# The odd layer's output projection: eight block products of its last 1024 columns against seven on sums of blocks

## The chip, the cores and the metric

The kernel runs on one core of a Trainium2 chip. The metric is device time in microseconds of one launch. Engine names are those of the profile: PE multiplies matrices (PEld loads its stationary operand), DVE, ACT and POOL work element by element (VectorE, ScalarE, GpSimd), and SP only issues transfers.

## The reference, cut to what matters

The reference is a two-layer encoder on 256 tokens of width 2048: an even layer with two attention branches, an odd layer with windowed attention, and a final norm. The change touches the last lines of the odd layer and the norm behind it:

```python
y = yc.reshape(b, s, C_WIDTH) * jax.nn.silu(gate)
h = h + jnp.einsum('bse,ed->bsd', y, w_out_odd[i])
...
return rms_norm(h, final_norm_g)
```

Here `y` is 256 x 2048 (tokens by features), `w_out_odd` is 2048 x 2048, and the norm divides each token's 2048 values by their root mean square and multiplies by a gain vector.

## The kernel before

Every projection is a *job*: 512 output columns for both halves of the tokens (`t` = 0, 1; 128 tokens each), accumulated over 16 feature tiles of 128 in two PSUM banks. A product in float32 accuracy is three matmuls (`mm3`, lines 186 to 188): each operand is held as a rounded high part and a low rest, and high*high, high*low and low*high are summed. So a job of 512 columns is 2 x 16 x 3 = 96 matmuls of 512 columns.

The weights come from memory as float32. `wgroup` (lines 131 to 150) loads one group, 128 x 1024 values (two feature tiles of 512 columns), into one of three `raw` buffers, ACT rounds it to `hi` (line 147) and DVE subtracts, `lo = raw - hi` (line 148). I call that pair a *split*. `hi` and `lo` have three buffers each, so ACT can begin the split of a group when PE has finished the group three places earlier. Each group feeds 12 matmuls.

The attention of the odd layer runs as small tasks between the groups. At the end of a head pair, `finish` multiplies the pair's outputs `o` by the gate (line 405), and splits them into the stationary operands `y[k]`, one for each of the 16 feature tiles. The output projection needs all of them, and the last four come late, so `two_jobs` (lines 211 to 217) runs columns 0 to 511 and 512 to 1023 side by side: the first six groups of both, then the last two of both. Sixteen groups in all; I number them w1 to w16 in the order in which PE takes them.

Behind them follow the columns 1024 to 1535 as a job of eight groups, the columns 1536 to 1791 as a job with 256 columns a matmul, and the columns 1792 to 2047 from weights split into tiles of the free activation pool `u`, once for each half of the tokens. After each job `final_add` (lines 744 to 749) adds the two PSUM banks to the residual stream `tok` on DVE, squares and sums it on ACT (line 244), and multiplies by the gain on DVE. When a token half has all its columns, lines 767 to 780 form the reciprocal root (one `pow` on POOL), scale the row on DVE and ACT, and write it out.

POOL issues the small transfers that turn activations by 128 (`turned`, line 287), and adds the attention bias tables (lines 425 and 427). Its last real work before the output projection is the `turned` transfers of the last two head pairs; in the output projection it has only the two `pow`.

The order on each engine is chosen at build time by the framework's scheduler from the program order; `tc.high_priority()` moves an instruction ahead of others, and `behind()` keeps an instruction behind the newest split.

## Time and profile before

| quantity | value |
|---|---|
| device time, median of 3 runs | 876.97 us (876.04 to 877.44) |
| device time of the profiled execution | 876.38 us |
| its span in the trace | 874.5 us |
| PE busy | 862.5 us, 99% |
| DVE busy | 650.9 us, 74% |
| ACT busy | 531.5 us, 61% |
| POOL busy | 283.4 us, 32% |
| granted PE clock, mean | 0.998 |

The span runs from the first to the last instruction of the trace; the launch around it is 1.9 us in the profiled execution, and the median of the runs is 0.6 us above that execution. Busy shares count an instruction from its start to its end, also while it waits for a port, and matmuls overlap each other, so a PE at 99% is one that is never without work, not one that has no faster way through it.

### The profile page before, as it was taken

The page shows a single profiled execution, that of the slowest core. Times are in us where ns is not written, and L with a number is a line of the kernel's source. Part 1 is how long each engine was busy: PE and PEld are TensorE (multiplying, and loading weights), DVE is VectorE, ACT ScalarE, POOL GpSimd, SP SyncE. Part 2 cuts the span into 40 slices and gives each one's busy share as a digit, 9 for nine tenths or more (in the row PEclk, how much of TensorE's full clock was granted, in tenths as well). Part 3 has the DMA queues.
Part 4 walks back from the last instruction along what each step waited for, and adds up shares of the span by engine and source line. Part 5 has one row for each costly group of instructions (what it writes and reads, how often), then busy time and mean ns, then how long its engine had stood idle before and what let it go on. Part 6 is the DMA issues. An engine that isn't in the chain of part 4 may idle for free. (4 is left out here: it accounts for less than half of the span.)

```text
span 874.5 us, 12145 instructions
## 1 busy us (share of the span) xinstructions
PE 862.5 (99%) x4068; PEld 722.8 (83%) x4068; DVE 650.9 (74%) x925; ACT 531.5 (61%) x882; POOL 283.4 (32%) x417
## 2 busy tenths in 40 slices
PE   8999999999999999999999999999999999999996
PEld 7788888888888888888888888888888888878896
DVE  6598879977997996786567875587658767785664
ACT  7755878769756964465455754475546655664542
POOL 0033323451555650322031732164115622450000
PEclk9999999999999999999999999999999999999999
DMA  8877564684667676667575666666665575576562
GB/s 299 296 260 241 184 228 160 205 263 165 193 195 250 218 247 213 197 223 255 197 229 183 219 214 217 212 196 217 214 219 193 183 245 175 186 259 233 192 203 108
DMA packets 58431, 187.75 MB, mean 215 GB/s; under 512 B 11072, under 2 KB 11840, under 8 KB 58368
## 3 DMA queue, kind: packets, MB, share of 16 engines
q1 hardware_dynamic: 46656, 162.57, 55.4%
q0 software_dynamic: 11712, 24.40, 9.3%
q8 instruction: 32, 0.52, 0.3%
q14 instruction: 31, 0.25, 0.1%
HBM read 161.50 MB, written 2.10 MB: 187 GB/s over the span
## 5 line engine op out<-in xcount | busy, mean ns | idle before, releaser
L148 DVE TENSOR_TENSOR lo<-raw,hi 128x1024 fp32r<-128x1024 f32 (+1 forms) x294 | 363.0, 1239 | 181.3 <-ACT hi L147 180.9
L147 ACT ACTIVATE hi<-raw 128x1024 fp32r<-128x1024 f32 (+1 forms) x294 | 309.4, 1053 | 266.1 <-PE acc_t L188 194.5
L187 PE MATMUL acc_t<-lo,u 128*128 128x512 f32 x928 | 361.3, 391 | 1.8 <-DVE lo L148 1.7
L188 PE MATMUL acc_t<-hi,u 128*128 128x512 f32 x928 | 360.5, 390 | 0.0
L186 PE MATMUL acc_t<-hi,u 128*128 128x512 f32 x928 | 332.7, 391 | 1.2 <-ACT u L232 1.2
L287 POOL DMA_DIRECT2D pt<-x x356 | 194.0, 596 | 329.4 <-DVE x L283 97.4
L187 PEld LDWEIGHTS acc_t<-lo,u 128*128 128x128 f32 x928 | 174.4, 188 | 38.2 <-DVE lo L148 3.9
L186 PEld LDWEIGHTS acc_t<-hi,u 128*128 128x128 f32 x928 | 173.3, 188 | 36.4 <-ACT u L232 2.3
L188 PEld LDWEIGHTS acc_t<-hi,u 128*128 128x128 f32 x928 | 174.4, 188 | 34.6
L187 PE MATMUL acc_t<-lo,y 128*128 128x512 f32 (+1 forms) x256 | 95.9, 376 | 0.0
L188 PE MATMUL acc_t<-hi,y 128*128 128x512 f32 (+1 forms) x256 | 95.8, 376 | 0.0
L425 POOL TENSOR_SCALAR bias<-geo 128x512 f32<-128x512 f32 x24 | 49.4, 2058 | 122.0 <-DVE s L420 115.4
L186 PE MATMUL acc_t<-hi,y 128*128 128x512 f32 (+1 forms) x256 | 87.0, 376 | 0.0
L188 PEld LDWEIGHTS acc_t<-hi,y 128*128 128x128 f32 x256 | 48.2, 188 | 8.7
L187 PEld LDWEIGHTS acc_t<-lo,y 128*128 128x128 f32 x256 | 48.1, 188 | 8.6
L186 PEld LDWEIGHTS acc_t<-hi,y 128*128 128x128 f32 x256 | 48.1, 188 | 8.6
L283 DVE STREAM_TRANSPOSE x<-z 128x256 f32<-128x256 f32 x82 | 45.0, 602 | 0.1
L283 DVE STREAM_TRANSPOSE x<-s 128x256 f32<-128x256 f32 x64 | 37.2, 620 | 7.4 <-ACT s L498 5.9
L368 ACT ACTIVATE s<-s,nm 128x256 f32<-128x256 f32 x64 | 31.7, 496 | 5.0 <-DVE nm L365 4.8
L265 ACT ACTIVATE z<-acc_t,rstd 128x512 f32<-128x512 f32 x40 | 27.0, 676 | 5.4 <-PE acc_t L188 5.3
L258 ACT ACTIVATE ph<-pt 128x512 fp32r<-128x512 f32 x32 | 19.9, 623 | 14.7 <-DMA pt<-x 14.6
L772 POOL TENSOR_TENSOR r<-r,nhalf 128x1 f32<-128x1 f32 x2 | 1.4, 679 | 78.8 <-DVE r L771 78.8
(138 smaller groups left out, 704.4 us busy)
## 6 DMA issues: line engine op xcount, KB each, us to landing
raw<-in_w_in_odd SPq DMA_DIRECT2D x128, 512.0 KB, 3.9
raw<-in_w_in_even SPq DMA_DIRECT2D x102, 512.0 KB, 3.8
pt<-x POOLq DMA_DIRECT2D x356, 64.0 KB, 3.5
raw<-in_w_out_even SPq DMA_DIRECT2D x32, 512.0 KB, 4.3
raw<-in_w_out_odd SPq DMA_DIRECT2D x32, 512.0 KB, 3.2
tok<-in_x SPq DMA_DIRECT2D x4, 512.0 KB, 8.3
xk<-in_xt SPq DMA_DIRECT2D x6, 256.0 KB, 5.2
raw<-in_w_in_even SPq DMA_DIRECT2D x4, 256.0 KB, 4.0
```

Source lines behind the costliest of these rows:

```text
L147: firsts.append(A.activation(hi[:, ks], rv[:, ks], AF.Copy))
L148: splits.append(V.tensor_sub(lo[:, ks], rv[:, ks], f(hi[:, ks])))
L186: T.matmul(ps, ah, bh, start=start, stop=False)
L187: T.matmul(ps, ah, bl, start=False, stop=False)
L188: T.matmul(ps, al, bh, start=False, stop=stop)
L258: A.activation(hi, src, AF.Copy)
L265: A.activation(z[:, t], ps[t], AF.Copy, scale=r[:, t:t + 1])
L283: V.transpose(x[:, :, 2 * m:2 * m + 2].rearrange("p b t c -> p t b c"), src[:, :, m * P:(m + 1) * P].rearrange("p t (r b) -> p t b r", b=4))
L287: G.dma_start(dst[:, a].rearrange("p n c -> p (n c)"), x[32 * a:32 * a + 32].rearrange("r b n c -> r (b n c)"))
L368: A.activation(e[:, t], s[:, t], AF.Exp, bias=nm[:, t:t + 1], accum_out=den[:, t:t + 1])
L425: G.tensor_scalar_mul(b, geo[:, 0], -slope)
L772: G.tensor_tensor(r, r, nhalf[:, :1], op=ALU.pow)
```

## The change

The columns 1024 to 2047 no longer run as three jobs. They are one product of 256 tokens x 2048 features with 2048 features x 1024 columns, cut into 2 x 2 blocks: tokens in two halves of 128, features in two halves of 1024, columns in two halves of 512. Three of the four pairs of feature tiles in each half (index `j` = 0, 1, 2) go through the seven-product scheme of Strassen and Winograd; the fourth pair of each half (feature tiles 6, 7, 14 and 15) is multiplied as before and closes the sums.

For each `j`, `strassen` loads four weight blocks of 128 x 1024 values (`b11`, `b12`, `b21`, `b22`) and makes seven right-hand sides: `b11`, `b21`, `b22` as they are, and four sums: `t1 = b12 - b11` (POOL), `t3 = b22 - b12` (POOL), `t3 + b11`, written over `b22` (DVE), and `b21` less that sum, written over `b21` (POOL). Each of the seven is split like a group before (ACT rounds, DVE subtracts) and feeds 6 matmuls of 512 columns. The left-hand sides are blocks of `y` or four sums of them (`left_forms`), made from the gated outputs `o` by four DVE instructions of 128 x 256 and one split of 128 x 1024 for each `j`; they are made while the first two jobs run, in the pool `u`.

The products' banks are added to `tok` when the last `j` is done: product 1 to both column halves of token half 0 by one DVE instruction; product 6 to one block by DVE; the other contributions by eight POOL additions of 128 x 512 from copies that ACT takes out of PSUM (`add_behind`). Products 2, 3 and 4 stay open and take the fourth pairs. The gain multiplication of columns 0 to 1535 moves from DVE to POOL (six instructions of 128 x 512), and that of columns 1536 to 2047 is merged into the last scaling on DVE. The weights of the first two `j` are loaded into attention tiles that are free by then. The gain vector's four transfers are issued after the twelfth group instead of before the first.

```diff
-CHUNKS_E = ((0, 512), (512, 512), (1024, 512), (1536, 512))
-CHUNKS = ((0, 512), (512, 512), (1024, 512), (1536, 256), (1792, 256))
+CHUNKS = ((0, 512), (512, 512), (1024, 512), (1536, 512))
...
-    def two_jobs(w, c0, c1, a, late=(6, 7)):
+    def two_jobs(w, c0, c1, a, late=(6, 7), between=None):
 
         ps = [job_banks(512) for _ in range(2)]
         for kgs in ([kg for kg in range(8) if kg not in late], late):
             for p, c in zip(ps, (c0, c1)):
                 job_steps(p, w, c, 512, a, kgs, last=2 * late[-1] + 1)
+            if kgs is not late and between:
+                between()
...
+    def left_forms(dst, a1, a2):
+        s = work.tile([P, 4, 2, P], F32, tag="z", name="s4", bufs=3)
+        a11, a21, a12, a22 = a1[:, :, :P], a1[:, :, P:], a2[:, :, :P], a2[:, :, P:]
+        V.tensor_add(s[:, 0], a21, a22)
+        V.tensor_sub(s[:, 1], s[:, 0], a11)
+        V.tensor_sub(s[:, 2], a11, a21)
+        V.tensor_sub(s[:, 3], a12, s[:, 1])
+        sv = s.rearrange("p f k c -> p f (k c)")
+        split(dst[:, :, 0], dst[:, :, 1], sv)
+    def strassen(wb, c0, c1, a, left, done):
+        w, where = wb
+        def load(c, kg, pool, tag, bufs):
+            dst = pool.tile([P, 1024], F32, tag=tag, name=f"w_{tag}", bufs=bufs)
+            loads.append(nc.sync.dma_start(dst, w[where[c] + kg]))
+            return dst
+        def load_three(j):
+            b11 = load(c0, j, heads, ("va", "ka")[j % 2], 1)
+            b12 = load(c1, j, heads, "k", 2)
+            b21 = load(c0, 4 + j, heads, "q", 2)
+            return b11, b12, b21
+        def first_form(b11, b12):
+            t1 = work.tile([P, 1024], F32, tag="z", name="t1", bufs=3)
+            with tc.high_priority():
+                G.tensor_sub(t1, b12, b11)
+            return t1
+        def parts_of(src):
+            count[0] += 1
+            if count[0] % 4:
+                hi = wpool.tile([P, 2, 512], F32R, tag="hi", name="hi")
+                lo = wpool.tile([P, 2, 512], F32R, tag="lo", name="lo")
+            else:
+                both = heads.tile([P, 2, 2, 512], F32R, tag="v", name="both", bufs=1)
+                hi, lo = both[:, 0], both[:, 1]
+            sv = src.rearrange("p (k c) -> p k c", k=2)
+            with tc.high_priority():
+                firsts.append(A.activation(hi, sv, AF.Copy))
+                splits.append(V.tensor_sub(lo, sv, f(hi)))
+            return hi, lo
+        count = [0]
+        three = load_three(0)
+        t1_next = first_form(*three[:2])
+        yield
+        b22_next = load(c1, 4, wpool, "raw", 3)
+        with tc.high_priority():
+            G.tensor_sub(three[1], b22_next, three[1])
+        ps = {i: bank() for i in (1, 2, 3, 5)}
+        ps.update({i: acc.tile([P, 512], F32, tag="acc", name=f"acc_s{i}") for i in (6, 7, 4)})
+        for j in range(3):
+            (b11, t3, b21), t1, b22 = three, t1_next, b22_next
+            def block(k0, t):
+                return lambda kk, i: a[k0 + 2 * j + kk][:, i, t * P:(t + 1) * P]
+            def form(n):
+                return lambda kk, i: left[j][:, n - 1, i, kk * P:(kk + 1) * P]
+            def product(i, lhs, rhs):
+                hi, lo = parts_of(rhs)
+                for kk in range(2):
+                    mm3(ps[i], lhs(kk, 0), lhs(kk, 1), hi[:, kk], lo[:, kk], j == kk == 0, i not in (2, 3, 4) and j == 2 and kk == 1)
+                if j == 2 and i not in (2, 3, 4):
+                    done(i, ps[i])
+            three = load_three(j + 1)
+            product(1, block(0, 0), b11)
+            product(2, block(8, 0), b21)
+            product(3, form(4), b22)
+            with tc.high_priority():
+                V.tensor_add(b22, t3, b11)
+                G.tensor_sub(b21, b21, b22)
+            b22_next = load(c1, 5 + j, wpool, "raw", 3)
+            if j < 2:
+                t1_next = first_form(*three[:2])
+            product(5, form(1), t1)
+            if j < 2:
+                with tc.high_priority():
+                    G.tensor_sub(three[1], b22_next, three[1])
+            product(7, form(3), t3)
+            product(6, form(2), b22)
+            product(4, block(8, 1), b21)
+        b11, b12, b21 = three
+        blocks = {b: parts_of(src) for b, src in (((0, 0), b11), ((1, 0), b21), ((0, 1), b12), ((1, 1), b22_next))}
+        end = {(0, 0): ps[2], (0, 1): ps[3], (1, 0): ps[4],
+               (1, 1): acc.tile([P, 512], F32, tag="acc", name="acc_s8")}
+        newest = None
+        for t, n in ((0, 0), (0, 1), (1, 0), (1, 1)):
+            for half in range(2):
+                hi, lo = blocks[half, n]
+                for kk in range(2):
+                    ak = a[8 * half + 6 + kk][:, :, t * P:(t + 1) * P]
+                    with tc.issue_after(newest.ins) if newest else nullcontext():
+                        newest = mm3(end[t, n], ak[:, 0], ak[:, 1], hi[:, kk], lo[:, kk],
+                                     t == n == 1 and half == kk == 0, half == kk == 1)
+            done((t, n), end[t, n])
...
+        gated[h // 2] = o
...
-    parts = small.tile([P, NT, 5], F32, tag="parts5", name="parts5", bufs=1)
-    gf = [acts.tile([P, 512], F32, tag="y", name="gf") for _ in range(4)]
-    for c in range(4):
-        G.dma_start(gf[c], final_g[c * 512:(c + 1) * 512].unsqueeze(0).to_broadcast([P, 512]))
-    def gfs(cs):
-        return gf[cs.start // 512][:, cs.start % 512:cs.start % 512 + cs.stop - cs.start]
-    def final_add(i, t, cs, ps, scaled=True):
+    parts = small.tile([P, NT, 4], F32, tag="parts4", name="parts4", bufs=1)
+    gf = []
+    def load_gf():
+        for c in range(4):
+            gf.append(acts.tile([P, 512], F32, tag="y", name="gf"))
+            G.dma_start(gf[c], final_g[c * 512:(c + 1) * 512].unsqueeze(0).to_broadcast([P, 512]))
+    forms = [None] * 3
+    def task_forms(j):
+        yield from until(lambda: gated[j] is not None and gated[j + 4] is not None)
+        yield 1
+        forms[j] = acts.tile([P, 4, 2, S], F32R, tag="u", name="forms", bufs=NK // UG)
+        with behind():
+            left_forms(forms[j], gated[j], gated[j + 4])
+    for j in range(3):
+        spawn(task_forms(j))
+    def columns_done(i, t, cs):
         z = tok[:, t, cs]
+        square_sum(parts[:, t, i:i + 1], z)
+        if i < 3:
+            G.tensor_mul(z, z, gf[cs.start // 512])
+    CS = slice(1024, 1536), slice(1536, 2048)
+    def rows_done(t):
+        ms = small.tile([P, NT], F32, tag="ss", name="ms")[:, :1]
+        V.reduce_sum(ms, parts[:, t, 0:3], axis=AX.X)
+        V.tensor_scalar(ms, ms, 1.0 / D, NORM_EPS, op0=ALU.mult, op1=ALU.add)
+        columns_done(3, t, CS[1])
+        r = small.tile([P, 8], F32, tag="r", name="r", bufs=2)[:, :1]
+        V.tensor_scalar(r, parts[:, t, 3:4], 1.0 / D, ms[:, 0:1], op0=ALU.mult, op1=ALU.add)
+        G.tensor_tensor(r, r, nhalf[:, :1], op=ALU.pow)
+        for c in (3, 0, 2, 1):
+            cs = slice(512 * c, 512 * c + 512)
+            z = tok[:, t, cs]
+            if c == 3:
+                V.scalar_tensor_tensor(z, z, r[:, 0:1], gf[c], op0=ALU.mult, op1=ALU.mult)
+            elif c == 2:
+                V.tensor_scalar_mul(z, z, r[:, 0:1])
+            else:
+                A.activation(z, z, AF.Copy, scale=r[:, 0:1])
+            nc.sync.dma_start(out2[t * P:(t + 1) * P, cs], z)
+    def add(t, n, ps):
+        z = tok[:, t, CS[n]]
         V.tensor_add(z, z, ps)
-        square_sum(parts[:, t, i:i + 1], z)
-        if scaled:
-            V.tensor_mul(z, z, gfs(cs))
-    for i, cs, ps in jobs_out(w_oo, CHUNKS[:4], y):
-        for t in range(NT):
-            final_add(i, t, cs, ps[t])
...
+    def add_both(t, ps):
+        z = tok[:, t, 1024:].rearrange("p (n c) -> p n c", n=2)
+        V.tensor_add(z, z, ps.unsqueeze(1).to_broadcast([P, 2, 512]))
+    def add_behind(ps, blocks):
+        m = work.tile([P, 512], F32, tag="s", name="m", bufs=3)
+        A.copy(m, ps)
+        for t, n in blocks:
+            z = tok[:, t, CS[n]]
+            G.tensor_add(z, z, m)
+    def product_done(i, ps):
+        if i == 1:
+            add_both(0, ps)
+            add_behind(ps, ((1, 0), (1, 1)))
+        elif i == 5:
+            add_behind(ps, ((0, 1), (1, 1)))
+        elif i == 7:
+            add_behind(ps, ((1, 0), (1, 1)))
+        elif i == 6:
+            add(0, 1, ps)
+            add_behind(ps, ((1, 0), (1, 1)))
+        else:
+            t, n = i
+            add(t, n, ps)
+            if n:
+                rows_done(t)
             else:
+                columns_done(2, t, CS[0])
+    steps = strassen(w_oo, 1024, 1536, y, forms, product_done)
+    for i, (cs, ps) in enumerate(zip((slice(0, 512), slice(512, 1024)), two_jobs(w_oo, 0, 512, y, between=lambda: (load_gf(), next(steps))))):
+        for t in range(NT):
+            V.tensor_add(tok[:, t, cs], tok[:, t, cs], ps[t])
+            columns_done(i, t, cs)
+    advance(lambda: all(x is not None for x in forms))
+    for _ in steps:
+        pass
```

Three places show what moved. In the rows that follow, `raw`, `w_raw`, `w_va`, `w_ka`, `w_k` and `w_q` are weight blocks as they were loaded, `t_7761` and its like are `t1`, `m` is a copy of a product's bank, and line numbers are those of the kernel they come from (the split of `wgroup` is L148 before and L147 after; that of `strassen` is L272).

POOL, from the last bias table of the attention to the end of the program, before:

```order
L427 TENSOR_TENSOR bias<-bias,geo 128x512
L287 DMA pt<-x 128x1x128 x12
L739 DMA gf<-in_final_norm_g 128x512 x4
L287 DMA pt<-x 128x1x128 x8
L772 TENSOR_TENSOR r<-r,nhalf 128x1 x2
```

POOL, from the same transfers to the eight additions, after:

```order
L395 DMA pt<-x 128x1x128 x20
L258 TENSOR_TENSOR t_7761<-w_k,w_va 128x1024
L258 TENSOR_TENSOR t_7901<-w_k,w_ka 128x1024
L853 DMA gf<-in_final_norm_g 128x512 x4
L281 TENSOR_TENSOR w_k<-w_raw,w_k 128x1024
L313 TENSOR_TENSOR w_k<-w_raw,w_k 128x1024
L871 TENSOR_TENSOR tok<-tok,gf 128x512 x4
L306 TENSOR_TENSOR w_q<-w_q,w_raw 128x1024
L258 TENSOR_TENSOR t_7982<-w_k,w_va 128x1024
L313 TENSOR_TENSOR w_k<-w_raw,w_k 128x1024
L306 TENSOR_TENSOR w_q<-w_q,w_raw 128x1024 x2
L909 TENSOR_TENSOR tok<-tok,m 128x512 x8
```

An engine that had two one-column instructions left now has nine of 128 x 1024 and twelve of 128 x 512 in these rows, and two more multiplications by the gain behind them, all with two inputs in SBUF.

DVE in the first two jobs, from the split of w3 to those of w5 to w7, before:

```order
L148 TENSOR_TENSOR lo<-raw,hi 128x1024
L405 TENSOR_TENSOR o<-o,pt 128x512
L274 SCALAR_TENSOR_TENSOR z<-th,z 128x512
L283 STREAM_TRANSPOSE x<-z 128x2x4x32 x4
L148 TENSOR_TENSOR lo<-raw,hi 128x1024
L259 TENSOR_TENSOR y<-o,y 128x256 x2
L148 TENSOR_TENSOR lo<-raw,hi 128x1024 x3
```

DVE in the same stretch, from the split of w3 to those of w5 and w6 (`s_7530` and `s_7538` are the sums for `j` = 0 and 1), after:

```order
L147 TENSOR_TENSOR lo<-raw,hi 128x1024
L234 TENSOR_TENSOR s_7530<-o,s_7530 128x256
L514 TENSOR_TENSOR o<-o,pt 128x512
L382 SCALAR_TENSOR_TENSOR z<-th,z 128x512
L147 TENSOR_TENSOR lo<-raw,hi 128x1024
L231 TENSOR_TENSOR s_7538<-o 128x256
L391 STREAM_TRANSPOSE x<-z 128x2x4x32 x4
L367 TENSOR_TENSOR forms<-s_7530,forms 128x4x256
L367 TENSOR_TENSOR y<-o,y 128x256 x2
L232 TENSOR_TENSOR s_7538<-s_7538,o 128x256
L147 TENSOR_TENSOR lo<-raw,hi 128x1024 x2
```

Three small instructions of the left-hand sums and the split of those for `j` = 0 (into `forms`) stand between the splits of w3 and w5; four more small ones stand ahead of w3, in rows not shown.

DVE from the last split of the first two jobs on, before:

```order
L746 TENSOR_TENSOR tok<-tok,acc_t_7481 128x512
L746 TENSOR_TENSOR tok<-tok,acc_t_7482 128x512
L148 TENSOR_TENSOR lo<-raw,hi 128x1024
L749 TENSOR_TENSOR tok<-tok,gf 128x512 x2
L148 TENSOR_TENSOR lo<-raw,hi 128x1024
```

DVE from the same additions on, after:

```order
L933 TENSOR_TENSOR tok<-tok,acc_t_7473 128x512
L933 TENSOR_TENSOR tok<-tok,acc_t_7474 128x512
L272 TENSOR_TENSOR lo<-w_va,hi 128x1024
L272 TENSOR_TENSOR lo<-w_q,hi 128x1024
L933 TENSOR_TENSOR tok<-tok,acc_t_7475 128x512
L933 TENSOR_TENSOR tok<-tok,acc_t_7476 128x512
L272 TENSOR_TENSOR lo<-w_raw,hi 128x1024
L305 TENSOR_TENSOR w_raw<-w_k,w_va 128x1024
L272 TENSOR_TENSOR lo<-w_k,hi 128x1024
L272 TENSOR_TENSOR lo<-w_raw,hi 128x1024
L272 TENSOR_TENSOR both<-w_ka,both 128x1024
L272 TENSOR_TENSOR lo<-w_q,hi 128x1024 x2
```

Where a split stood for 12 matmuls there is now one for six, and one sum of weight blocks for each `j` between them.

## Rows read from the trace of the kernel before

**Rows 1.** The page, part 1: busy time, share of span, instructions.
```profile
PE 862.5 (99%) x4068; PEld 722.8 (83%) x4068; DVE 650.9 (74%) x925; ACT 531.5 (61%) x882; POOL 283.4 (32%) x417
```

**Rows 2.** Windows (stretch, length, busy by engine, PEclk, DMA share, GB/s).
```profile
777.20:821.50 44.30, 44.30 (x199) 36.77 (x198) 31.00 (x39) 23.51 (x34) 4.40 (x9) 1.00 0.67 233
821.50:843.30 21.80, 21.80 (x98) 18.06 (x97) 12.25 (x13) 9.83 (x12) 0.00 (x0) 1.00 0.57 194
866.50:874.50 8.00, 0.00 (x0) 0.00 (x0) 2.24 (x6) 1.23 (x3) 0.67 (x1) 0.77 0.42 153
```

**Rows 3.** Chain that ended last (start us, us, what): group beginnings, fifteen groups apart.
```profile
799.91 0.45 PE acc_t L186 x2
...
840.71 0.45 PE acc_t L186 x2
```

**Rows 4.** Timeline of PE (start, us, instruction): 256-column pace, last matmul.
```profile
850.10 0.28 PE L186 MATMUL acc_t<-hi,y 128*128 128x256 f32 x1
...
850.46 0.28 PE L186 MATMUL acc_t<-hi,y 128*128 128x256 f32 x1
...
866.18 0.28 PE L188 MATMUL acc_l<-u,y 128*128 128x256 f32 x1
```

**Rows 5.** Timeline of PE: the first matmuls of w5.
```profile
788.87 0.62 PE L186 MATMUL acc_t<-hi,y 128*128 128x512 f32 x2
789.32 0.39 PE L187 MATMUL acc_t<-lo,y 128*128 128x512 f32 x1
```

**Rows 6.** Timeline of DVE in the first two jobs: splits of w2, w3, w5/w6, w16.
```profile
777.30 1.23 DVE L148 TENSOR_TENSOR lo<-raw,hi 128x1024 fp32r<-128x1024 f32 x1 [0.24 <-ACT hi L147]
778.44 0.76 DVE L259 TENSOR_TENSOR y<-o,y 128x256 fp32r<-128x256 f32 x2
...
780.10 1.23 DVE L148 TENSOR_TENSOR lo<-raw,hi 128x1024 fp32r<-128x1024 f32 x1 [0.25 <-ACT hi L147]
...
786.47 2.36 DVE L148 TENSOR_TENSOR lo<-raw,hi 128x1024 fp32r<-128x1024 f32 x2
...
814.64 1.23 DVE L148 TENSOR_TENSOR lo<-raw,hi 128x1024 fp32r<-128x1024 f32 x1 [1.49 <-ACT hi L147]
```

**Rows 7.** Timeline of DVE in the attention, where POOL worked at the same time.
```profile
477.89 2.10 DVE L148 TENSOR_TENSOR lo<-raw,hi 128x1024 fp32r<-128x1024 f32 x1 [1.13 <-ACT hi L147]
...
596.18 1.22 DVE L148 TENSOR_TENSOR lo<-raw,hi 128x1024 fp32r<-128x1024 f32 x1 [0.24 <-ACT hi L147]
...
671.17 1.17 DVE L283 STREAM_TRANSPOSE x<-s 128x256 f32<-128x256 f32 x2
...
682.33 2.54 DVE L148 TENSOR_TENSOR lo<-raw,hi 128x1024 fp32r<-128x1024 f32 x1 [0.52 <-ACT hi L147]
```

**Rows 8.** Timeline of POOL at the same times.
```profile
477.62 1.30 POOL L427 TENSOR_TENSOR bias<-bias,geo 128x512 f32<-128x512 f32 x1
...
596.78 1.76 POOL L427 TENSOR_TENSOR bias<-bias,geo 128x512 f32<-128x512 f32 x1
...
671.32 1.36 POOL L427 TENSOR_TENSOR bias<-bias,geo 128x512 f32<-128x512 f32 x1
...
682.43 1.35 POOL L427 TENSOR_TENSOR bias<-bias,geo 128x512 f32<-128x512 f32 x1
```

**Rows 9.** The instructions of line 427: ns min/median/max, first and last start.
```profile
L427 POOL TENSOR_TENSOR bias<-bias,geo x16: 1285/1353/1919, 251.3 to 756.6; 128x512 f32<-128x512 f32 x16
```

**Rows 10.** Timeline of POOL in the first two jobs: the last `turned` transfers.
```profile
784.02 4.32 POOL L287 DMA_DIRECT2D pt<-x  x8 [6.74 <-DVE x L283]
```

**Rows 11.** Timeline of all engines behind the last matmul.
```profile
866.50 0.42 DVE L746 TENSOR_TENSOR tok<-tok,acc_l 128x256 f32<-128x256 f32 x1 [2.40 <-PE acc_l L188]
867.01 0.42 ACT L244 ACTIVATE sq<-tok 128x256 f32<-128x256 f32 x1 [3.46 <-DVE tok L746]
```

**Rows 12.** Groups by line and shape, from 780 us on (count, busy us, mean ns).
```profile
L746 DVE TENSOR_TENSOR tok<-tok,acc_t 128x512 f32<-128x512 f32 x6 | 3.8, 680 | 0.0
...
L244 ACT ACTIVATE sq<-tok 128x512 f32<-128x512 f32 x6 | 3.7, 624 | 0.1
```

More of the change, by code (lines that the diff above doesn't have):

```diff
@@ L1 @@
 import math
-from contextlib import ExitStack, contextmanager
+from contextlib import ExitStack, contextmanager, nullcontext
 import numpy as np
@@ L71, in job_columns @@
         return quads[:11] + quads[12:15] + quads[11:12] + quads[15:]
-    return list(CHUNKS_E if name == "out_even" else CHUNKS)
+    return list(CHUNKS)
 def blocked(w, name):
@@ L187, in mm3 @@
         T.matmul(ps, ah, bl, start=False, stop=False)
-        T.matmul(ps, al, bh, start=False, stop=stop)
+        return T.matmul(ps, al, bh, start=False, stop=stop)
     def job_banks(wd):
@@ L346, in trunk @@
     y = [None] * NK
+    gated = [None] * (NK // 2)
     def bank():
@@ L674, in trunk @@
     un = [None] * NK
-    for i, cs, ps in jobs_out(w_oe, CHUNKS_E, y_even, (2, 3)):
+    for i, cs, ps in jobs_out(w_oe, CHUNKS, y_even, (2, 3)):
         for t in range(NT):
@@ L684, in trunk @@
     y = [None] * NK
+    gated = [None] * (NK // 2)
     oc = []
@@ L751, in trunk @@
-    for i, cs, ps in jobs_out(w_oo, CHUNKS[:4], y):
-        for t in range(NT):
-            final_add(i, t, cs, ps[t])
-    wl = [acts.tile([P, UG, 2, S], F32R, tag="u", name="u", bufs=NK // UG) for _ in range(NK // UG)]
-    for kg in range(NK // UG):
-        wgroup(w_oo, D - S, S, kg, into=(wl[kg][:, :, 0], wl[kg][:, :, 1]))
-    for t in range(NT):
-        ts = slice(t * P, (t + 1) * P)
-        ps = acc.tile([P, 512], F32, tag="acc", name="acc_l")[:, :S]
-        for k in range(NK):
-            wk = wl[k // UG][:, k % UG]
-            mm3(ps, y[k][:, 0, ts], y[k][:, 1, ts], wk[:, 0], wk[:, 1], k == 0, k == NK - 1)
-        cs = slice(D - S, D)
-        final_add(4, t, cs, ps, False)
-        ms = small.tile([P, NT], F32, tag="ss", name="ms")[:, :1]
-        V.reduce_sum(ms, parts[:, t, 0:4], axis=AX.X)
-        V.tensor_scalar(ms, ms, 1.0 / D, NORM_EPS, op0=ALU.mult, op1=ALU.add)
-        r = small.tile([P, 8], F32, tag="r", name="r", bufs=2)[:, :1]
-        V.tensor_scalar(r, parts[:, t, 4:5], 1.0 / D, ms[:, 0:1], op0=ALU.mult, op1=ALU.add)
-        G.tensor_tensor(r, r, nhalf[:, :1], op=ALU.pow)
-        V.tensor_mul(tok[:, t, cs], tok[:, t, cs], gfs(cs))
-        for c0, c1, eng in ((0, 256, V), (256, 768, A), (768, 1280, V), (1280, D, V)):
-            z = tok[:, t, c0:c1]
-            if eng is A:
-                A.activation(z, z, AF.Copy, scale=r[:, 0:1])
-            else:
-                V.tensor_scalar_mul(z, z, r[:, 0:1])
-            nc.sync.dma_start(out2[ts, c0:c1], z)
```

1 line of the change is left out of this document (added).

## The prediction

> **What bounds the kernel now.** I read the busy shares first, then the windows over the output projection, then the timelines of PE, DVE and POOL. PE is busy 99% of the span [rows 1]. In the output projection it is never without work, from 777.2 us to its last matmul at 866.2, and its clock is granted in full [rows 2, 4]. DVE is busy 31.0 of the 44.3 us of the first two jobs and 12.3 of 21.8 us in the job behind them; POOL does nothing in that job [rows 2]. So PE sets the pace here, with room on DVE and an idle POOL. The question is whether the work that replaces 18 matmuls fits into that room.
>
> **Matmuls removed.** Fifteen groups of 12 matmuls take 40.80 us, 2.72 a group, 0.2267 a matmul of 512 columns [rows 3]. Three matmuls of 256 columns take 0.36 us, 0.120 each [rows 4]. The columns 1024 to 2047 cost 96 x 0.2267 + 192 x 0.120 = 21.8 + 23.0 = 44.8 us. Afterwards there are 3 x 7 x 6 = 126 matmuls of 512 columns in the products and 48 for the fourth pairs: 174 x 0.2267 = 39.4 us. If PE still set the pace, that is 5.4 us less.
>
> **The end.** From the last matmul's end (866.46) to the end of the span are 8.0 us. The chain there now works on 512 columns instead of 256: an addition of 0.68 instead of 0.42 us and a square of 0.62 instead of 0.42 [rows 11, 12]. With 0.1 for scalings in equal pieces I take 0.6 us more, 8.6. Nothing hides it; between none and 1.0 it matters little.
>
> **What POOL's work costs DVE.** This is the term that decides. A split by itself takes 1.23 us, and a second right behind it ends 1.13 us after the first [rows 6]. In the attention, the split that started at 477.89 took 2.10 us. POOL's addition beside it ended at 478.92, the split at 479.99, 1.07 us later. The split at 682.33 took 2.54 us; POOL's addition ended at 683.78, the split 1.09 us behind it [rows 7, 8]. DVE stood until POOL was almost done and then did its whole work. The trace has eight such meetings, all alike. The other way round, POOL's addition at 596.78 took 1.76 us instead of 1.29 behind the split of 596.18 [rows 7 to 9]. Two transposes, which read one input, took 1.17 us for both beside POOL's addition at 671.32, and that took its usual 1.36 [rows 7, 8]. So a DVE instruction with two inputs in SBUF and a POOL addition exclude each other. A POOL addition of 512 columns holds DVE up for 1.30 - 0.15 = 1.15 us; a split holds POOL up for about 1.13.
>
> Nothing in the trace shows POOL on 1024 columns. Bounds: no dearer than 512 columns (1.15), or twice the slower median, 2 x 1.353 - 0.15 = 2.56 [rows 9]. I take twice the shortest, 2 x 1.285 - 0.15 = 2.42, as the work is twice as much. The Trainium skill, "GPSIMD Engine Reference", section 3.1, gives 4497 ns for such an addition of 2048 columns; half of it, an estimate, is 2.25 us; no row here shows it. By that figure the nine instructions below would cost 1.5 us less together.
>
> **First two jobs.** PE must have the low part of w5 at 789.32 [rows 5]. Its split ended at 786.47 + 1.23 = 787.70 [rows 6]. Ahead of it DVE now has seven small sums of 128 x 256 (0.34 each, from two in 0.76 with 0.42 for the first) and one split of the left-hand sums: 7 x 0.34 + 1.13 = 3.5 us, of which 0.5 falls into the waits of 0.24 and 0.25 ahead of w2 and w3 [rows 6]. w5 is ready at 790.7, and PE waits 1.4 us. POOL's first two sums come right behind its last transfers; these ended at 788.3 [rows 10], and now follow transposes that are 3.0 us later: at about 791. DVE then does w6 (to 791.8), stands 2.42, does a small sum, stands 2.42 again, and has w7 at 798.1. PE wants it at 789.32 + 1.4 + 2 x 2.72 = 796.2, and waits 1.9. Another split of left-hand sums and an `o` product stand before w8 (0.2 of waiting), five small sums and a product before w9 (0.7). Together 4.2 us, between 1.4 (POOL free of charge) and 4.5. Behind w9 the splits wait for PE anyhow, and DVE's room hides the rest. The extra weight loads of this stretch I cost at nothing: DMA is busy 0.67 of it [rows 2]. The gain's transfers, which move behind w12, give back some of that. If that cover is gone, a load of 512 KB late by a microsecond costs about that.
>
> **From the last split of the first two jobs to the last split of all.** The split of w16 ended at 815.87 [rows 6]. Add 4.2, and 2.42 for the first `t3`, which POOL makes just then: 822.5. From here both engines have more work than time. For one `j` DVE has seven splits and one sum, POOL three sums: 8 x 1.13 + 3 x 2.42 = 16.3 us that exclude each other, where PE needs 7 x 6 x 0.2267 = 9.5. ACT's part runs beside it. So PE waits for the queue in front of DVE and POOL, and the time to the last split is its sum:
> 24 splits and 3 sums on DVE, 27 x 1.13 = 30.5;
> 6 sums of 1024 columns on POOL (`t3` for `j` = 1, `t1` and `t3` for `j` = 2, three `b21`), 6 x 2.42 = 14.5;
> 4 gain multiplications on POOL, 4 x 1.15 = 4.6, ahead of the first `b21` in its queue;
> 6 of the 8 additions to `tok` on POOL, 6 x 1.15 = 6.9.
> The first three of those additions come before the last two splits by force: DVE adds product 6 ahead of these splits, and waits there for the addition of product 5. The other three fall between the splits. The sum is 56.5 us; the last split ends at 879.0.
>
> **Behind it** PE still has 30 of the 48 closing matmuls, 6.8 us with 0.1 for the hand-over: 885.9. With 8.6 for the end the span is 894.5 us, 20.0 more than 874.5. Device time lay 1.9 us above the span in the profiled execution, and the median of the runs 0.6 above that; both carry over. 876.97 + 20.0 = 897.0. So 5.4 us of PE's time are bought with about 25 of waiting.
>
> **Rivals.** *POOL and DVE do not exclude each other here* (another kind of tile, another timing). Then PE waits only 1.4 us in the first two jobs: 821.5 + 1.4 + 39.4 + 8.6 = 870.9, 3.6 less, 873.4 us: not slower, and faster by 0.4%. DVE has 30.5 us and some 4 for reading banks in that stage, under PE's 39.4, so PE keeps the pace. It decides if POOL's instructions cost DVE less than about 0.2 us each. The eight meetings speak against it. Chance 0.10.
> *DVE goes first whenever both wait.* Then the six additions slip behind the last split, which ends at 872.1, and PE at 879.0. But the eight additions take 8 x 1.30 = 10.4 us alone, to 882.5, and the last rows wait for them: 882.5 + 8.6 = 891.1, or 893.6 us. The trace has no place where both queue, so it says nothing against it. Chance 0.15.
> *PE's clock falls.* PE will stand 2 us and more between bursts of six matmuls. The clock was granted in full while PE had work, and 0.77 on the mean over the last 8 us, when it had stopped [rows 2]; there it went to the lower of its levels, 1.2 GHz. If the closing matmuls run at half speed, 6.8 us are added: 904 us. If the whole stage does, PE needs 174 x 0.453 = 78.9 us from 825.7 on, and 916 us come out. The Trainium skill, "TensorE: Matmul & The Clock Gate", section "Why this matters for your kernels", warns against idle gaps between bursts for this reason; the row agrees as far as it goes. Chance 0.13.
>
> **How the numbers follow.** The forecast, 897.0 us, has 0.62. Its own bounds: if POOL's nine sums cost 1.15 each, 11.4 less, 885.6; at 2.56 and with 0.1 us lost in each of some 30 hand-overs, 4.3 more, 901. The range of 886 to 908 holds the forecast, the second rival and the milder half of the third; the first rival (0.10) and the worst of the third (0.06) are left out. A measurement of this kernel tells about 0.2% (1.8 us) from no change. Faster by more than that: most of the first rival, 0.07. Within it: 0.03. Slower: 0.90.
>
> **What would show it.** In the profile after: PE idle some 30% of the stage behind the first two jobs, ended by DVE's `lo` of line 272; splits there of 2.2 to 3.7 us instead of 1.23, each with a POOL instruction inside; POOL's instructions of 1024 columns at 2.5 us by themselves and longer behind DVE; a stall at w5 and one at w7; DVE and POOL together busy without a gap. Wrong it would be if splits beside POOL take 1.23, if POOL's sums of 1024 columns take near 1.3, or if PE's clock row leaves 9 in the last slices.

## The result

The changed kernel takes 897.2 us (median of 4 runs, 896.2 to 898.5), the kernel before 876.5 beside it: a ratio of 1.0231 [1.0218, 1.0244], 20.7 us slower. The forecast was 897.0. Its profiled execution took 896.18 us with a span of 894.3; the launch around it is 1.9 us as before.

From the page of the changed kernel, busy time (answers to [rows 1]), and from its windows (columns as in [rows 2]) the first two jobs, the stage from the split of w16 to the last split's end, the matmuls behind it, and the end:

```profile
PE 864.4 (97%) x3954; PEld 714.0 (80%) x3954; DVE 694.6 (78%) x940; ACT 545.7 (61%) x896; POOL 340.0 (38%) x440
```

```profile
777.20:821.50 44.30, 40.77 (x181) 33.03 (x180) 39.15 (x50) 24.88 (x33) 16.61 (x15) 1.00 0.65 214
820.40:878.10 57.70, 44.31 (x171) 31.79 (x169) 56.76 (x35) 29.22 (x36) 45.26 (x18) 0.97 0.24 81
878.10:885.10 7.00, 6.87 (x29) 5.37 (x29) 3.58 (x10) 3.51 (x8) 4.33 (x5) 1.00 0.18 61
885.10:894.30 9.20, 0.00 (x0) 0.00 (x0) 2.10 (x5) 2.06 (x4) 1.67 (x2) 0.71 0.56 181
```

In the second stretch DVE is busy 56.8 of 57.7 us and PE 44.3: PE stands 13.4 us, where it stood for nothing in the kernel before [rows 2]. What it waits for, from PE's list of waits from 777 us on (us in total, times, the longest; the row of `acc_t` is from the first two jobs):

```profile
PE acc_s L186 <- DVE lo L272: 5.7, 5, 1.7
PE bank L186 <- DVE lo L272: 3.6, 4, 1.7
PE acc_t L186 <- DVE lo L147: 3.5, 2, 2.1
PE acc_s L185 <- ACT hi L271: 1.8, 2, 1.3
PE bank L186 <- DVE both L272: 1.7, 2, 1.2
PE acc_s L186 <- DVE both L272: 0.6, 1, 0.6
```

All but one are low parts from DVE. The row of ACT goes back to DVE as well: ACT was rounding a block that DVE's own sum (line 305) had only just finished, as ACT's timeline shows for the longer of the two waits:

```profile
832.24 1.06 ACT L271 ACTIVATE hi<-w_raw 128x1024 fp32r<-128x1024 f32 x1 [1.69 <-DVE w_raw L305]
```

And DVE is busy because it stands inside its instructions. From DVE's timeline of that stage (start, us):

```profile
836.49 3.40 DVE L272 TENSOR_TENSOR both<-w_ka,both 128x1024 fp32r<-128x1024 f32 x1
839.92 6.63 DVE L272 TENSOR_TENSOR lo<-w_q,hi 128x1024 fp32r<-128x1024 f32 x2
...
847.62 1.21 DVE L272 TENSOR_TENSOR both<-w_k,both 128x1024 fp32r<-128x1024 f32 x1
...
861.28 1.21 DVE L901 TENSOR_TENSOR tok<-tok,bank 128x1024 f32<-128x1024 f32 x1
...
869.07 2.30 DVE L272 TENSOR_TENSOR lo<-w_ka,hi 128x1024 fp32r<-128x1024 f32 x1
```

And from POOL's, the same stage:

```profile
820.74 2.40 POOL L281 TENSOR_TENSOR w_k<-w_raw,w_k 128x1024 f32<-128x1024 f32 x1 [16.59 <-DMA w_raw<-in_w_out_odd]
...
826.45 9.04 POOL L871 TENSOR_TENSOR tok<-tok,gf 128x512 f32<-128x512 f32 x4
835.45 3.35 POOL L306 TENSOR_TENSOR w_q<-w_q,w_raw 128x1024 f32<-128x1024 f32 x1
838.77 3.38 POOL L258 TENSOR_TENSOR t<-w_k,w_va 128x1024 f32<-128x1024 f32 x1
842.22 3.25 POOL L313 TENSOR_TENSOR w_k<-w_raw,w_k 128x1024 f32<-128x1024 f32 x1
...
863.58 16.90 POOL L909 TENSOR_TENSOR tok<-tok,m 128x512 f32<-128x512 f32 x8
```

A split with no POOL instruction near it takes 1.21 us (847.62). Beside an addition of 512 columns it takes 2.3 (869.07), beside a sum of 1024 columns 3.3 to 3.4 (836.49, and two in 6.63 from 839.92). POOL's sum takes 2.40 where nothing holds it up (820.74) and 3.25 to 3.4 beside splits; four gains take 9.04 where [rows 9] has 1.35 for one. From 863.58 on the two engines take turns, an addition and a split about every 2.2 us.

The span falls into three stretches, marked by the start of DVE's part of the first and sixteenth split, PE's last matmul's end, and the end of the span. Later tables use the same marks (us; profiled executions, whose w1 starts between 774.6 and 776.0):

| kernel | w1 to w16 | w16 to last matmul | last matmul to end |
|---|---|---|---|
| before | 40.0 | 51.8 | 8.0 |
| after | 44.2 | 65.8 | 9.3 |

So of 19.8 us in the span, 4.2 come in the first two jobs, 14.0 in the new stage, 1.3 at the end and 0.3 before w1. The 14.0 are 5.2 us of matmuls saved, as experiment e5 shows below, and about 19 of waiting. PE is idle for 13.4 us of these. The rest lies, as far as the rows show, in the matmuls' own pace: behind a wait they start 0.34 us apart (as at 878.13) where 0.227 is usual, and for 3.5 us they ran at the lower clock (see the third rival below).

### The profile page after: what moved, and what is told of

It is laid out like the page before. It is cut to its first block, busy times and chain, and to the rows that moved or that the text cites. A ratio compares the mean times of both kernels' runs of the same rounds, so it can differ in the third digit from the quotient of the medians.

```text
span 894.3 us, 11980 instructions
## 1 busy us (share of the span) xinstructions
PE 864.4 (97%) x3954; PEld 714.0 (80%) x3954; DVE 694.6 (78%) x940; ACT 545.7 (61%) x896; POOL 340.0 (38%) x440
## 5 line engine op out<-in xcount | busy, mean ns | idle before, releaser
L147 DVE TENSOR_TENSOR lo<-raw,hi 128x1024 fp32r<-128x1024 f32 (+1 forms) x282 | 350.1, 1247 | 162.5 <-ACT hi L146 162.0
L146 ACT ACTIVATE hi<-raw 128x1024 fp32r<-128x1024 f32 (+1 forms) x282 | 296.8, 1053 | 250.4 <-PE acc_t L187 180.5
L186 PE MATMUL acc_t<-lo,y 128*128 128x512 f32 x192 | 74.7, 391 | 3.5 <-DVE lo L147 3.5
L187 PE MATMUL acc_t<-hi,y 128*128 128x512 f32 x192 | 74.2, 389 | 0.0
L185 PE MATMUL acc_t<-hi,y 128*128 128x512 f32 x192 | 66.9, 389 | 0.0
L186 PEld LDWEIGHTS acc_t<-lo,y 128*128 128x128 f32 x192 | 36.0, 188 | 12.0 <-DVE lo L147 4.6
L187 PEld LDWEIGHTS acc_t<-hi,y 128*128 128x128 f32 x192 | 36.0, 188 | 7.3
L185 PEld LDWEIGHTS acc_t<-hi,y 128*128 128x128 f32 x192 | 35.9, 188 | 7.4
L367 DVE TENSOR_TENSOR pl<-pt,ph 128x512 fp32r<-128x512 f32 x32 | 25.0, 781 | 3.4 <-ACT ph L366 3.3
```

The source lines that it names most:

```text
L146: firsts.append(A.activation(hi[:, ks], rv[:, ks], AF.Copy))
L147: splits.append(V.tensor_sub(lo[:, ks], rv[:, ks], f(hi[:, ks])))
L185: T.matmul(ps, ah, bh, start=start, stop=False)
L186: T.matmul(ps, ah, bl, start=False, stop=False)
L187: return T.matmul(ps, al, bh, start=False, stop=stop)
L367: V.tensor_sub(lo, src, f(hi))
```

## Experiments

**Is it POOL's work that DVE stands for?** Four kernels take POOL's new work away in parts. The first leaves the nine sums of weight blocks out (`t1`, `t3` and `b21` keep a block as it was loaded):

```diff
-                G.tensor_sub(t1, b12, b11)
-            return t1
+            return b12
...
-            G.tensor_sub(three[1], b22_next, three[1])
...
-                G.tensor_sub(b21, b21, b22)
```

> The nine sums of weight blocks on POOL are left out (the blocks themselves take their places in the products); everything else stays, DVE's 24 splits and 3 sums too. Theory 1 (a DVE instruction with two inputs in SBUF and a POOL addition exclude each other, and their common queue is what the new stage waits for): the queue loses 7 x 2.42 = 16.9 us and the first two jobs 2.8 us of waiting, so 877 us (874 to 881). Rival (DVE's own load, one split for six matmuls and few buffers, is what the stage waits for; POOL only runs beside it): DVE has as much to do as before, 897 us.

Measured 882.75 us, a ratio of 1.0071 [1.0056, 1.0086], above the 874 to 881 that were expected: the nine sums cost 14.5 us. Without them the splits also need not wait for POOL's results, so this run alone does not tell exclusion from POOL's own length. The second leaves out POOL's eight additions to `tok` and its six gains:

```diff
-            G.tensor_mul(z, z, gf[cs.start // 512])
+            pass
...
-            G.tensor_add(z, z, m)
+            pass
```

> The eight additions to the residual stream and the six gain multiplications on POOL are left out; the nine weight sums stay. Theory 1 (common queue of DVE and POOL): ten of these fourteen stand in the queue with 1.15 us each, so 11.5 us less than 897, 886 us (883 to 889). Rival (DVE's own load): 897 us.

Measured 889.3 us, 1.0142 [1.0127, 1.0157]: 8 us, just above the range that was expected. The third leaves both out, by the two edits above together:

> Weight sums, additions and gain multiplications on POOL are all left out; DVE keeps its 24 splits and 3 sums and all the rest. Theory 1 (common queue): what is left is PE's own time, 1.4 us of waiting in the first two jobs and 39.4 us for 174 matmuls: 873.4 us (872 to 876), the time at which the change would have been faster than the kernel before. Rival (DVE's own load): 897 us.

Measured 876.68 us, 0.9993 [0.9984, 1.0003]: 20.5 us less than the changed kernel, nearly the 14.5 and 8 together, and 0.7 above the range that was expected. DVE's new instructions are all still there, so its own load does not cost the 20 us; what it does cost comes with e7 below. Each split is back at its time alone, as DVE's timeline of this kernel shows in the stretch of additions:

```profile
854.14 0.68 DVE L888 TENSOR_TENSOR tok<-tok,acc_s 128x512 f32<-128x512 f32 x1
854.74 1.22 DVE L269 TENSOR_TENSOR lo<-w_q,hi 128x1024 fp32r<-128x1024 f32 x1
```

The fourth keeps all results and gives the nine sums to DVE instead of POOL:

```diff
-                G.tensor_sub(t1, b12, b11)
+                V.tensor_sub(t1, b12, b11)
```

(and so for `t3` and `b21`).

> The nine sums of weight blocks are made by DVE instead of POOL; the result is the same. Theory 1 (common queue): each sum takes 1.13 us of the queue on DVE instead of 2.42 on POOL, nine of them 11.6 us less: 886 us (882 to 889), although DVE gets 10 us more work. Rival (DVE's own load): 10 us more on the engine that the stage waits for, 907 us.

Measured 892.86 us, 1.0180 [1.0163, 1.0197], 4 us above the range that was expected. The kernel is faster although the engine that PE waits for has more work: the rival of DVE's load falls here too. The gain is 4.4 us where 11 were expected. A sum costs DVE 1.13 us when it runs it, so on POOL it had cost in effect, by this estimate, (9 x 1.13 + 4.4) / 9 = 1.6 us and not 2.42; e1 gives the same, 14.5 / 9. The next experiments say why in part. In this profiled execution PE's clock was granted only 0.91 on the mean from 820 to 880 us; DVE was busy throughout the stretches in which it was low, so no loss to the clock shows.

**All of it on DVE.** Beside the sums, the additions (straight from the banks) and the gains:

```diff
-        m = work.tile([P, 512], F32, tag="s", name="m", bufs=3)
-        A.copy(m, ps)
...
-            G.tensor_add(z, z, m)
+            V.tensor_add(z, z, ps)
```

> All that the change gave POOL goes to DVE: nine sums, eight additions to tok (straight from the bank, without ACT's copy) and six multiplications by the gain. Theory 1: from the 892.86 us with the sums alone on DVE some 10.6 us of blocked time go, and 8 x 0.6 + 4 x 0.57 = 7.1 us of DVE work come: 889.4, 886 to 892. Rival (DVE's own load decides, POOL costs it little): DVE has 7 us more, so about 900.

Measured 889.05 us, 1.0137 [1.0120, 1.0153], as expected. It is the fastest of the kernels here that compute the seven-product scheme whole, and still 12 us behind the kernel before.

**The price by itself.** Only instructions of the disputed kinds, in stretches with a barrier between them. In outline:

```diff
+    for i in range(6):
+        G.tensor_sub(g[i], a, b)
+    for i in range(12):
+        V.tensor_sub(lo[i % 8], src[i % 8], hi[i % 8])
+    stop()
```

> The price by itself: nothing of the reference is computed, only instructions of the disputed kinds, in stretches with a barrier between them. Alone: POOL 1024 columns with two inputs 2.4 us, 512 columns 1.3; DVE 1024 columns 1.23, the next 1.13 later. Theory 1 (two inputs in SBUF on both sides exclude each other): six POOL sums of 1024 columns beside twelve DVE subtractions need the sum of both, 6 x 2.3 + 12 x 1.13 = 27.4 us, as against 14 if they overlap; eight POOL additions of 512 columns beside twelve subtractions 8 x 1.15 + 13.6 = 22.8. Open within theory 1 is who goes first when both are queued: in strict turns each DVE instruction meets one POOL instruction (3.3 to 3.5 us each while POOL lasts); if DVE keeps the port as long as it has work without a gap, POOL's first instruction ends after DVE's twelfth. A DVE instruction with one operand in a bank, one with a single input, and a POOL instruction with a single input are expected to run beside the other engine at their times alone. Rival (DVE's own load, no exclusion): every pair of lists takes the time of the longer one.

Its groups by line and shape (count, busy us, mean ns): alone on lines 43 to 58, and then in pairs, lines 62 with 64, 68 with 70, 74 with 76, 80 with 82, 86 with 88.

```profile
L64 DVE TENSOR_TENSOR lo<-src,hi 128x1024 f32<-128x1024 f32 x12 | 26.6, 2286 | 0.2 <-SPq L59 0.2
L70 DVE TENSOR_TENSOR lo<-src,hi 128x1024 f32<-128x1024 f32 x12 | 22.2, 1924 | 0.1
...
L62 POOL TENSOR_TENSOR g<-a,b 128x1024 f32<-128x1024 f32 x6 | 19.8, 3327 | 10.3 <-SPq L59 10.3
L82 DVE TENSOR_SCALAR lo<-src 128x1024 f32<-128x1024 f32 x16 | 18.3, 1216 | 0.1
...
L88 DVE TENSOR_TENSOR lo<-src,hi 128x1024 f32<-128x1024 f32 x12 | 17.1, 1493 | 0.1
...
L49 POOL TENSOR_SCALAR g<-a 128x1024 f32<-128x1024 f32 x4 | 11.0, 2771 | 0.2 <-SPq L47 0.2
L76 DVE TENSOR_TENSOR lo<-src,bank 128x512 f32<-128x512 f32 x16 | 9.7, 681 | 0.1
...
L43 POOL TENSOR_TENSOR g<-a,b 128x1024 f32<-128x1024 f32 x4 | 9.2, 2340 | 23.0 <-SPq L40 23.0
...
L52 DVE TENSOR_TENSOR lo<-src,hi 128x1024 f32<-128x1024 f32 x4 | 4.6, 1220 | 25.9 <-SPq L50 25.9
L58 DVE TENSOR_SCALAR lo<-src 128x1024 f32<-128x1024 f32 x4 | 2.5, 688 | 0.2 <-SPq L56 0.2
L55 DVE TENSOR_TENSOR lo<-src,bank 128x512 f32<-128x512 f32 x4 | 2.5, 683 | 0.1
```

Twelve subtractions one behind the other take 13.7 us (four in 4.63, so 1.14 more for each). Beside six POOL sums they take 26.6: each sum holds DVE up for 12.9 / 6 = 2.15 us, just under its own 2.34. An addition of 512 columns costs (22.2 - 13.7) / 8 = 1.07 us. So the exclusion holds at 1024 columns, and the two engines take turns from the start: a sum every 3.3 us. The sixteen additions with one operand in a bank take 9.7 us beside POOL, as long as alone (2.5 for four), so those run beside POOL for nothing.

Two expectations fell. One is about POOL and comes with the next kernel. The other: a DVE instruction with one input is not always spared. Sixteen multiplications take 0.60 us each by themselves and 18.3 us beside four POOL sums; four of them were held, for (18.3 - 9.7) / 4 = 2.15 us each, as a subtraction is. "Two inputs in SBUF", the prediction's words, are thus not the whole condition. The Trainium skill, "SBUF — State Buffer", section "Who interferes with whom", says both: two SBUF inputs contend with a POOL instruction that reads SBUF, and one-input operations contend where they run in a mode that uses both of DVE's ports, which `tensor_scalar` can. The rows agree on who is held; whether the multiplications ran in such a mode no row says, only that 1024 columns took them 0.60 us where a subtraction takes 1.14.

**POOL with one input.** The sums become multiplications of one block by 0.5, of the same size:

```diff
-                G.tensor_sub(t1, b12, b11)
+                G.tensor_scalar_mul(t1, b12, 0.5)
```

> POOL's nine sums of weight blocks become nine multiplications of one block by 0.5, same size, same engine, same buffers (the seven products then multiply the wrong right-hand sides). If POOL blocks DVE by its second input only, this goes to where the kernel without the sums went, 882.75 us: 882 to 885. If any POOL instruction that reads and writes SBUF blocks DVE, it stays with the changed kernel, 895 to 898. If it is POOL's own length that PE waits for, and not DVE's, the time follows the length of the multiplications: near 897 when they take 2.4 us.

Measured 889.84 us, 1.0148 [1.0128, 1.0167], between the three expectations, so none of them holds. The price list explains it: beside twelve subtractions a one-input multiplication cost (17.1 - 13.7) / 4 = 0.85 us (lines 88 and 52), though it takes 2.74 itself. It holds DVE for a third of its time. The same is seen in this kernel, in DVE's timeline and in POOL's:

```profile
842.57 2.05 DVE L272 TENSOR_TENSOR both<-w_k,both 128x1024 fp32r<-128x1024 f32 x1
```

```profile
841.60 3.69 POOL L306 TENSOR_SCALAR w_q<-w_q 128x1024 f32<-128x1024 f32 x1 [0.56 <-DVE lo L272]
```

The split is 0.82 us longer than alone. The time thus does not follow POOL's own length, which grew; it goes with the time for which POOL keeps DVE out. How much of the 7.4 us gained comes from that is not shown, because a multiplication also has no second block to wait for.

**Where do the 5.4 us of matmuls go?** Without any of POOL's work (e5) the change only breaks even. The next kernel leaves out the left-hand sums and their splits on DVE as well (ACT's part of these splits goes too); products that used them take blocks of `y`:

```diff
-            left_forms(forms[j], gated[j], gated[j + 4])
+        V.memset(forms[j][:, 0, 0, 0:2].bitcast(F32), 0.0)
```

> The kernel without any of POOL's new work (876.68 us), and also without the left-hand sums and their splits on DVE (products that used them take blocks of y). Theory 1: the stretch from the split of w1 to that of w16 took 42.95 us there and 40.02 in the kernel before; without these instructions it goes back to about 40, so 874.0, 873 to 875.5. What is left over the 871 that PE's matmuls alone would give is DVE, whose 27 long instructions and bank additions leave no gap in the new stage. Rival: the extra weight loads hold that stretch up, not DVE: then 876.7 as before.

Measured 874.20 us, 0.9969 [0.9958, 0.9980], as expected. The three stretches:

| kernel | w1 to w16 | w16 to last matmul | last matmul to end |
|---|---|---|---|
| before | 40.0 | 51.8 | 8.0 |
| without POOL's work (e5) | 42.9 | 46.7 | 9.2 |
| and without left-hand sums (e7) | 40.4 | 46.9 | 9.3 |

The new stage does save 5.2 us (51.8 - 46.7). The left-hand sums take back 2.5 of it and the end 1.2; in e5's profiled execution w1 also started 1.4 us later than before, in e7's too, and no run shows why. The extra weight loads are still in e7, where w1 to w16 is 0.4 longer than before: by themselves they cost next to nothing. PE's longest wait in e5's first two jobs is this one (PE's timeline); in e7 it is not there:

```profile
792.86 0.73 PE L185 MATMUL acc_t<-hi,y 128*128 128x512 f32 x2 [1.41 <-ACT hi L146]
793.76 0.50 PE L186 MATMUL acc_t<-lo,y 128*128 128x512 f32 x1 [0.17 <-DVE lo L147]
```

ACT's high part came late because its weights did (ACT had waited 2.83 us for them, to 791.75). But DVE's low part, which PE needed next, was ready only at 793.7, so the transfer alone does not explain the wait.

Even in e5 the stage is close to its other bound. Its window of 20.8 us:

```profile
824.20:845.00 20.80, 20.80 (x94) 17.21 (x93) 20.11 (x19) 15.55 (x18) 0.00 (x0) 1.00 0.50 162
```

DVE is busy 20.1 of 20.8 us with POOL standing still, against 12.3 of 21.8 before [rows 2]. There is no room for anything that makes DVE wait.

The same edit in the changed kernel, with POOL's work whole:

> The changed kernel without the left-hand sums and their splits on DVE; POOL's work stays whole (products that used the sums take blocks of y). Theory 1: they cost about what they cost without POOL's work, 876.68 - 874.20 = 2.5 us, somewhat more if DVE's waits for POOL in the first two jobs came from them: 892.5 to 895. Rival: they are hidden beside POOL's blocking, and the time stays at 897. Of the 20.7 us that the change costs, this part then is a small one either way.

Measured 896.04 us, 1.0209 [1.0192, 1.0226], between the two expectations. It is 1.2 us below the changed kernel, but the interval overlaps that kernel's [1.0218, 1.0244]. The order on POOL shifts too: its first two sums run before the last transfers, a DVE instruction of 512 columns takes 6.45 us beside them (at 772.14), and w1 starts 3.6 us later than in the changed kernel. So what the left-hand sums cost beside POOL's work is not shown.

**Who goes first?** In the changed kernel POOL's first sum stood long in the first two jobs. POOL's timeline, then DVE's:

```profile
791.59 6.13 POOL L258 TENSOR_TENSOR t<-w_k,w_va 128x1024 f32<-128x1024 f32 x1
797.67 3.40 POOL L258 TENSOR_TENSOR t<-w_k,w_ka 128x1024 f32<-128x1024 f32 x1
```

```profile
789.87 2.37 DVE L147 TENSOR_TENSOR lo<-raw,hi 128x1024 fp32r<-128x1024 f32 x2
792.14 0.44 DVE L234 TENSOR_TENSOR s<-o,s 128x256 f32<-128x256 f32 x1
792.47 1.24 DVE L147 TENSOR_TENSOR lo<-raw,hi 128x1024 fp32r<-128x1024 f32 x1
...
794.21 1.24 DVE L367 TENSOR_TENSOR forms<-s,forms 128x1024 fp32r<-128x1024 f32 x1
795.75 3.04 DVE L147 TENSOR_TENSOR lo<-raw,hi 128x1024 fp32r<-128x1024 f32 x1 [0.31 <-ACT hi L146]
798.72 2.63 DVE L231 TENSOR_TENSOR s<-o 128x256 f32<-128x256 f32 x1
```

DVE ran on until 795.4, stopped 0.31 us for ACT, and then POOL got through: 797.72 - 2.34 = 795.4. Two lists of instructions were to show whether a run under way on DVE, the transfers ahead on POOL, or a shape on DVE keeps POOL out. The first, in outline (in other stretches eight transfers stand for the fills, or another operation for the subtractions):

```diff
+    for i in range(2):
+        G.memset(e, 1.0)
+    for i in range(4):
+        G.tensor_sub(g[i], a, b)
+    for i in range(14):
+        V.tensor_sub(lo[i % 8], src[i % 8], hi[i % 8])
```

> Nothing of the reference is computed. In the first list of prices, with both lists queued at once, POOL and DVE took strict turns (POOL 3.3 us a sum); in the changed kernel POOL's first sum stood 3.8 us at 791.6 while DVE ran five instructions. Here POOL comes to its first sum when DVE's run has already begun: behind two fills (1.8 us), or behind eight transfers. If a run that is under way keeps the port, POOL's first sum ends only behind DVE's last instruction in the stretches with fills and with transfers, some 14 to 16 us. If the transfers hold POOL up by themselves, its first sum takes 3 us more behind them alone and the usual 3.3 behind fills. If small instructions in between (256 columns) matter, the third stretch differs from the first. Of the other DVE kinds: copies of 1024 columns, one input, are expected to be blocked like the one-input multiplications (2.2 us for each POOL sum), transposes not, and ACT's copies not.

The second, in outline (or `turns()`, eight transfers between SBUF tiles, for the fills):

```diff
+    def run():
+        form(0)
+        ys(0)
+        small(1)
+        plain(2)
+        small(2)
+        plain(1)
+        gate(3)
+        form(1)
+    fills(3)
+    sums(2)
+    run()
+    run()
```

> Nothing of the reference is computed. In the stretches with 1024 columns on both sides POOL's first sum was never held up for more than one DVE instruction, in the changed kernel it was, for 3.8 us. Here DVE runs the very shapes of that place (the split of the left-hand sums into forms, two y splits of 128 x 256, small sums, three splits, a multiplication by the gate), and POOL comes behind transfers between SBUF tiles or behind fills. If one of these shapes keeps POOL out, its first sum takes over 5 us in the stretch with fills and in one of the two that hold a part of the shapes. If the transfers do it, in the two stretches with transfers only. If neither, all first sums take 2.3 to 3.5 us, and the cause at 791.6 stays open.

None of them does. In the first list POOL's first sum behind fills took its turn within one DVE instruction. Behind transfers POOL was not held at all:

```profile
56.64 9.22 POOL L54 TENSOR_TENSOR g<-a,b 128x1024 f32<-128x1024 f32 x4
```

Four sums took 9.22 us there, as long as alone (line 43 above), so DVE stood for all four in a row. The second had DVE's very shapes; POOL behind fills, POOL behind transfers, and the DVE row beside the latter:

```profile
53.11 6.12 POOL L53 TENSOR_TENSOR g<-a,b 128x1024 f32<-128x1024 f32 x2
...
74.58 4.74 POOL L53 TENSOR_TENSOR g<-a,b 128x1024 f32<-128x1024 f32 x2
```

```profile
74.47 5.14 DVE L66 TENSOR_TENSOR z<-src 128x256 f32<-128x256 f32 x1
```

Here it is DVE that stood for two POOL sums in a row, 4.7 us. In all three stretches of the two lists in which POOL came behind transfers, its sums ran in a row (9.22, 4.73 and 4.74 us); from a common start and behind fills the engines mostly took turns. Yet in the changed kernel POOL came behind transfers too, and there it was POOL that stood. So turns are not a law, and why POOL stood for 3.8 us at 791.6 stays open. In the first list also: twelve transposes took 4.04 us beside three sums of 2.34 each, and ACT's copies 1.04 us each with POOL at 2.35, so neither meets POOL; twelve plain copies on DVE took 13.75 us beside three sums, which took 2.8 each (no run has the copies alone).

## Why the prediction was right, step by step

The total is within 0.3 us (20.7 us slower than the kernel beside it, 20.0 forecast), and the mechanism was the one that was forecast: POOL's sums and additions hold DVE's splits up, and PE waits for the splits. Several terms were off.

- **Matmuls, -5.4 us**: right. e5 shows -5.2.
- **First two jobs, 4.2 us**: the sum is right (40.0 to 44.2), its parts are not. PE waited 1.39 us at w5 as forecast, but not at w7; the other wait, 2.15 us, came at w9, because POOL's first two sums held DVE up at 795.75 and 798.72 and not from 791.8 on. And by e5 the larger part, 2.9 us, is there without POOL, 2.5 of it from the left-hand sums; but e5 makes the first `t1` split 20 us earlier (785.08, not 804.69), so the parts need not add up. PE's waits explain 3.5 of the 4.2 us; the rest is not taken apart. Behind w9 ACT's parts of w12 to w15 waited for their weights (0.65 to 2.93 us) and not for PE; no wait of PE's came of it, so the loads that were costed at nothing did cost nothing there.
- **The first `t3` ahead of the split of w16**: wrong. That split ended at 820.4, not 822.5; `t3` ran behind it. 2.1 us too many.
- **The price of a sum**: 2.42 us held were forecast, 2.15 measured. The lower estimate that stands beside it in the prediction is a sum's own length and was set against a time held; less the same 0.15 it would have made the nine sums 2.9 us cheaper and not 1.5.
- **The queue, 56.5 us**: measured 57.7, from 820.4 to 878.1. Its 27 long DVE instructions are right, 30.7 us. POOL's part was put at 26.0; the rows of DVE, each less its time alone, add up to 21.3. Two reasons: a sum holds DVE for 2.15 us, not 2.42, and where POOL ran beside a bank addition or a pause of DVE it cost nothing (the addition at 861.28 took 1.21 with POOL's `b21` beside it). Left out of the sum were DVE's bank additions, 4.1 us, which the prediction had hidden under PE's time in its first rival alone, and 1.6 us that are left over (DVE is idle for 0.9 of them). These misses cancel but for 1.2.
- **Behind the last split, 6.9 us**: right (878.1 to 885.0).
- **The end, 8.6 us**: 9.3. The last addition and square are as costed; 0.7 more lie behind the last scalings.

Together 820.4 + 57.7 + 6.9 + 9.3 = 894.3, forecast 822.5 + 56.5 + 6.9 + 8.6 = 894.5. That the total came so close is luck: misses of up to 4.7 us cancel in it. What was right is the mechanism and the size of most terms.

Of the rivals, the first (no exclusion) falls with m1 and e5. The second (DVE goes first) falls in the stretch that it named: the eight additions alternated with the splits, and the chain that ended last runs over them (start, us, what):

```profile
860.36 2.81 POOL w_q L306
863.17 0.40 issue
863.58 11.30 POOL tok L909 x6
```

The third (the clock) came in a harmless form. One window of the stage and PE's timeline within it:

```profile
830.00:840.00 10.00, 6.92 (x22) 4.73 (x20) 9.96 (x5) 3.72 (x6) 10.00 (x5) 0.83 0.34 111
```

```profile
836.28 0.63 PE L187 MATMUL acc_s<-hi,forms 128*128 128x512 f32 x1
836.71 0.63 PE L185 MATMUL bank<-both,y 128*128 128x512 f32 x1
```

PE had stood for 1.34 us and, one matmul later, for 0.57 (ends at 833.35 and 834.41); the clock was granted 0.83 on the mean of these 10 us, and the matmuls followed 0.43 us behind each other, near twice the 0.227 of [rows 3], as at 1.2 GHz. From 837.91 on they are 0.23 us apart again, as at 2.4 GHz. DVE was busy for 9.96 of these 10 us, and the next matmuls then waited 1.17 us for it, so the lower clock cost nothing that shows in the end; from 840 on the clock was granted in full, though PE went on standing between bursts.

## What to carry to other kernels

A count of matmuls saved is worth only what the engines that feed them have to spare: here 5 us of PE time asked for over 50 us of two-input work on DVE and POOL, which turned out to be one resource. Before giving elementwise work to an idle POOL, look in the trace for one DVE instruction that ran beside one POOL instruction, and take its stretched time as the price; DVE instructions that read a bank, or transposes, are the ones to put beside POOL. And take a kernel's pieces away one by one, since a right total can hide terms that cancel.
